# Gate and up projections of two 768-token feed-forwards as seven half products each, with the down projection cut into pieces between them

## The chip, the cores and the metric

The program runs on one core of one Trainium2 chip. The metric is the time of one execution on the device, in microseconds (us); lower is better. The core has TensorE (PE in the rows; its weight loads are PEld), VectorE (DVE), ScalarE (ACT), GpSimd (POOL) and the queue SP, from which most transfers are issued.

## What is computed

The reference is two blocks of two layers each over 512 tokens of width 1024, with 256 context tokens beside them. Each of the four layers ends in a feed-forward of hidden width 2816:

```python
def swiglu(h, w_in, w_out):
    g, u = jnp.split(h @ w_in, 2, axis=-1)
    return (jax.nn.silu(g) * u) @ w_out
```

In the first layer of each block the kernel runs the feed-forward over the 512 tokens and the 256 context tokens together (768 columns); in the second layer of each block over 512. All arithmetic is float32.

## The kernel before, in words

Activations lie with the model dimension on the 128 partitions: eight tiles of 128 x tokens. A float32 product is made of three passes of TensorE: each operand is split into a rounded part `hi` and the rest `lo`, and `mm3` adds hi·hi, hi·lo (of the activations) and lo·hi (of the weights) into one accumulator in PSUM. `segs` cuts 768 columns into a matmul of 512 and one of 256, each with its own weight load.

The hidden width is 22 chunks of 128. For a chunk c, `ffn` calls `chunk` twice (gate and up): `wload` transfers 128 x 1024 weights into a `wraw` tile (4 buffers), ScalarE writes `whi` (L298) and GpSimd `wlo` (L299; 3 buffers each), and 8 x 3 x 2 matmuls follow (L306, L308, L310). Then ScalarE makes silu of the gate (L683), VectorE multiplies it by the up result in PSUM (L684), and `split` makes the hidden pair (L334 on ScalarE, L335 on VectorE). Chunks stand in groups, two in the first and four in each of five others. After the first chunk of the next group, `down` multiplies a group's hidden pairs by its rows of the down projection: one `wload` holds 8 blocks of 128 x 128, and each of the 8 output tiles takes 6 matmuls for each hidden chunk and is then added into the residual by VectorE (L574, one instruction for 512 columns and one for 256). PSUM gives three accumulators of two banks (`pd`); two more banks (`pq`) are for small things.

During these feed-forwards VectorE also computes the modulation vectors of the next layer (`ada`, L372): 48 weight tiles go through the same `wraw` buffers, with one or two multiply-and-sum instructions each, doled out by `fill.pace()`.

The order of the instructions of an engine is made by a list scheduler: the order in the program is the priority, and a later instruction may go first when it is ready earlier. On the chip each engine keeps that order.

Of the kernel before, what the change touches and what calls it, by code (L numbers as in the profile page):

```python
# [21 lines left out]
P = 128  # L22
# [195 lines left out]
class Kern:  # L218
# [110 lines left out]
    def split(self, src, n, lo_eng=None, pool=None):  # L329
# [301 lines left out]
    def ffn(self, x, wg, wu, wo, h, m, g, n, st, norm, fill, parts):  # L631

        nc = self.nc
        hp = self.es.enter_context(self.tc.tile_pool(name=self.nm("hid"), bufs=8, reuse_waits="tile"))
        oi = 0
        end = len(FGROUPS) - 1

# [35 lines left out]
        before = None  # L673
        for gi, grp in enumerate(FGROUPS):
            hid = []
# [469 lines left out]
    def ffn_block(self, a, win, wout, l, h, m, g, n, st, norm, fill=None, parts=None):  # L1145
        wi, wo = self.I[win], self.I[wout]
        self.ffn(a, lambda c: wi[l * 44 + c], lambda c: wi[l * 44 + 22 + c], lambda c: wo[l * 22 + c], h, m, g, n, st, norm, fill or Fill(), parts)

# [11 lines left out]
    def layer0(self):  # L1160
# [4 lines left out]
        with ExitStack() as es:  # L1165
            self.psum(es, pd=1, sc=2)
            w = I["even_w_in"]
            with self.tc.tile_pool(name="raw", bufs=6, reuse_waits="tile") as pool:
                a, ws = self.first_modulated(job, load, [w[8], w[12], w[16]], pool)
            for n in ("lamv", "cos", "sin", "sguw", "sgub"):  # L1170
                self.nc.sync.dma_start(getattr(self, n), I[n])
            self.ada_vectors(0)
            y = self.even_mixer(a, ws)
            st, h, a = self.stat(T, False), [], self.pairs()
            norm = self.rms_modulated(a, h, T, st, "norm2_g0", m, 24, 32)
            self.out_proj(I["even_w_out"], y, [4, 5, 6, 7, 0, 1, 2, 3], load, m, 16, T, h, st, norm)
            self.dump("hm0", h, T)
        with ExitStack() as es:
            self.psum(es, pd=3)
            st, b = self.stat(T, False), self.pairs()  # L1180
# [6 lines left out]
    def layer1(self, h, a, job):  # L1187
# [12 lines left out]
        with ExitStack() as es:  # L1200
            self.psum(es, pd=3)
            st = self.stat(NL, False)
# [668 lines left out]
    def second(self, h, st, job):  # L1871
# [3 lines left out]
        with self.es2 as es0:  # L1875
# [9 lines left out]
            with ExitStack() as es:  # L1885
                self.psum(es, pd=3)
                job = self.ada_start(1, 1)
# [18 lines left out]
            with ExitStack() as es:  # L1906
                self.psum(es, pd=3)
                st = self.stat(NL, True)
# [49 lines left out]
    def block1(self):  # L1958
        nc, tc, I = self.nc, self.tc, self.I
        with ExitStack() as es:  # L1960
# [5 lines left out]
            self.sin = self.t(bc, [P, NL], "sin")  # L1966
            self.sguw = self.t(bc, [P, 4, P], "sguw")
            self.sgub = self.t(bc, [P, 4, P], "sgub")
            self.lamv = self.t(bc, [64, 4], "lamv")
# [10 lines left out]

def lay_out(w):
    out = []
    w4 = w.reshape(-1, P, KC, P)
    for grp in FGROUPS:
        nk = len(grp)
# [48 lines left out]
def layout(x):  # L2034
# [11 lines left out]
    a["ffn_w_in"] = np.concatenate([lay_in(f["ffn_w_in"][l]) for l in range(2)])  # L2046
    a["ffn_w_out"] = np.concatenate([lay_out(f["ffn_w_out"][l]) for l in range(2)])
    a["cos"], a["sin"] = rope_tables()
# [72 lines left out]
```

## Time and profile before

| what | value |
|---|---|
| median of 3 runs | 4047.41 us (4041.08 to 4049.92) |
| the profiled execution | 4058.61 us, its span 4056.8 us |
| mean granted clock of TensorE | 0.944 of full speed |
| TensorE busy | 3690.5 us, 91% of the span |
| VectorE, GpSimd, ScalarE busy | 55%, 34%, 33% |
| feed-forward of 768 tokens, first block | from about 461 to 1020 us of the span |
| the same, second block | from about 2640 to 3200 us |

Busy time of an engine is the time in which an instruction of it runs; matmuls are pipelined, so their spacing, not their duration, says how fast they go. The rows below are from the profiled execution, and its numbers stand against its own 4058.61 us, which is 11 us above the median.

### The profile page before, as it was taken

The page shows a single profiled execution, that of the slowest core. Times are in us where ns is not written, and L with a number is a line of the kernel's source. Part 1 is how long each engine was busy: PE and PEld are TensorE (multiplying, and loading weights), DVE is VectorE, ACT ScalarE, POOL GpSimd, SP SyncE. Part 2 cuts the span into 40 slices and gives each one's busy share as a digit, 9 for nine tenths or more (in the row PEclk, how much of TensorE's full clock was granted, in tenths as well). Part 3 has the DMA queues.
Part 4 walks back from the last instruction along what each step waited for, and adds up shares of the span by engine and source line. Part 5 has one row for each costly group of instructions (what it writes and reads, how often), then busy time and mean ns, then how long its engine had stood idle before and what let it go on. Part 6 is the DMA issues. An engine that isn't in the chain of part 4 may idle for free.

```text
span 4056.8 us, 57267 instructions
## 1 busy us (share of the span) xinstructions
PE 3690.5 (91%) x22809; PEld 3065.6 (76%) x22809; DVE 2233.0 (55%) x4199; ACT 1347.2 (33%) x2337; POOL 1388.1 (34%) x804
## 2 busy tenths in 40 slices
PE   6989999999799899998977869699999899989997
PEld 4777788888677778776755657688888777778886
DVE  4784554333776676646767664755333654364225
ACT  5542212112466222243332322331111365543222
POOL 2112322222312444432332224552222542245443
PEclk9999999999899999989886879899999899999998
DMA  5124134333101255424445768223333221222331
GB/s 194 37 96 155 56 104 129 119 113 118 48 27 53 89 181 172 151 82 129 125 135 154 220 185 278 81 68 120 115 119 121 77 64 60 61 73 78 94 99 57
DMA packets 263002, 450.18 MB, mean 111 GB/s; under 512 B 63504, under 2 KB 168592, under 8 KB 259664
## 3 DMA queue, kind: packets, MB, share of 16 engines
q1 hardware_dynamic: 257536, 424.50, 33.7%
q10 hardware_dynamic: 5200, 22.02, 1.6%
q8 instruction: 180, 2.95, 0.3%
q14 instruction: 86, 0.70, 0.1%
HBM read 383.02 MB, written 63.44 MB: 110 GB/s over the span
## 4 chain that ended last, share of the span: by engine, by line
PE 38%; DVE 7%; DMA 2%; ACT 2%; issue 1%; POOL 1%; SPq 0%; ACTq 0%; DVEq 0%; POOLq 0%
PE pd L310 9%; PE pd L306 9%; PE pd L308 9%; PE pq L982 1%; DVE s L181 1%; DVE h L171 1%; PE ch L1756 1%; POOL s L1491 1%; PE sc L1135 1%; PE c L1513 1%; PE pq L997 1%; PE ch L1743 1%; PE sc L1138 1%; DVE h L557 0%; DMA lf<-ldd 0%
## 5 line engine op out<-in xcount | busy, mean ns | idle before, releaser
L299 POOL TENSOR_TENSOR wlo<-wraw,whi 128x1024 fp32r<-128x1024 f32 (+2 forms) x406 | 937.5, 2311 | 1916.8 <-ACT whi L298 1801.7
L306 PE MATMUL pd<-s,whi 128*128 128x512 f32 (+1 forms) x3481 | 1055.1, 356 | 37.4 <-ACT s L509 10.0
L308 PE MATMUL pd<-s,whi 128*128 128x512 f32 (+1 forms) x3421 | 1044.8, 356 | 14.7 <-DVE s L510 6.4
L310 PE MATMUL pd<-s,wlo 128*128 128x512 f32 (+1 forms) x3481 | 1053.3, 354 | 1.6 <-POOL wlo L299 1.6
L298 ACT CAST whi<-wraw 128x1024 fp32r<-128x1024 f32 (+2 forms) x414 | 405.6, 981 | 1627.3 <-PE pd L308 924.9
L306 PEld LDWEIGHTS pd<-s,whi 128*128 128x128 f32 x3481 | 585.9, 191 | 141.4 <-ACT s L509 12.2
L310 PEld LDWEIGHTS pd<-s,wlo 128*128 128x128 f32 x3481 | 589.7, 191 | 94.1 <-POOL wlo L299 3.5
L308 PEld LDWEIGHTS pd<-s,whi 128*128 128x128 f32 x3421 | 577.1, 191 | 109.5 <-DVE s L510 9.7
L372 DVE SCALAR_TENSOR_TENSOR junk<-wraw,cond 128x1024 bf16<-128x1024 f32 x160 | 263.8, 1649 | 395.5 <-DMA wraw<-in_ada_w 395.2
L574 DVE SCALAR_TENSOR_TENSOR h<-pd,mod,h 128x512 f32<-128x512 f32 (+1 forms) x323 | 196.2, 636 | 200.8 <-PE pd L310 200.4
L684 DVE TENSOR_TENSOR s<-s,pd 128x768 f32<-128x768 f32 (+1 forms) x88 | 71.9, 817 | 344.5 <-PE pd L310 310.3
L306 PE MATMUL pd<-hid,whi 128*128 128x512 f32 (+1 forms) x624 | 194.8, 350 | 4.9 <-DVE h L574 4.2
L308 PE MATMUL pd<-hid,whi 128*128 128x512 f32 (+1 forms) x624 | 194.0, 348 | 1.2 <-DVE hid L335 1.2
L310 PE MATMUL pd<-hid,wlo 128*128 128x512 f32 (+1 forms) x624 | 192.9, 347 | 0.0
L954 DVE TENSOR_REDUCE negm<-sc 128x1 f32<-128x512 f32 (+1 forms) x128 | 96.3, 754 | 118.3 <-PE sc L1135 107.4
L372 DVE SCALAR_TENSOR_TENSOR wraw<-wraw,cond 128x1024 f32<-128x1024 f32 x96 | 129.1, 1345 | 4.0
L306 PEld LDWEIGHTS pd<-hid,whi 128*128 128x128 f32 x624 | 110.4, 193 | 22.5 <-DVE h L574 2.4
L308 PEld LDWEIGHTS pd<-hid,whi 128*128 128x128 f32 x624 | 110.8, 194 | 16.3 <-DVE hid L335 1.7
L306 PE MATMUL pd<-in,whi 128*128 128x256 f32 (+1 forms) x384 | 114.0, 363 | 9.9 <-DVE h L1228 7.9
L310 PEld LDWEIGHTS pd<-hid,wlo 128*128 128x128 f32 x624 | 110.9, 194 | 15.3
L181 DVE TENSOR_TENSOR s<-s,s 128x256 f32<-128x256 f32 (+2 forms) x106 | 101.4, 957 | 37.6 <-ACT s L180 36.2
L308 PE MATMUL pd<-in,whi 128*128 128x256 f32 (+1 forms) x384 | 114.3, 365 | 2.9 <-POOL in L510 1.9
(375 smaller groups left out, 5761.6 us busy)
## 6 DMA issues: line engine op xcount, KB each, us to landing
wraw<-in_ada_w SPq DMA_DIRECT2D x160, 512.0 KB, 3.6
wraw<-in_ffn_w SPq DMA_DIRECT2D x132, 512.0 KB, 3.6
wraw<-in_ffn_w_in SPq DMA_DIRECT2D x88, 512.0 KB, 3.6
wraw<-in_ffn_w_out SPq DMA_DIRECT2D x44, 512.0 KB, 3.6
recd<-xr SPq DMA_DIRECT2D x72, 256.0 KB, 2.9
rec<-recd ACTq DMA_DIRECT2D x12, 1536.0 KB, 7.8
rec<-recd SPq DMA_DIRECT2D x12, 1536.0 KB, 7.0
raw<-in_ada_w SPq DMA_DIRECT2D x32, 512.0 KB, 5.8
```

The lines of the kernel that those rows point to most:

```text
L171: nc.vector.tensor_tensor(out=x[:, a:b], in0=x[:, a:b], in1=self.shift[:, a:b], op=ALU.subtract)
L181: nc.vector.tensor_tensor(out=self.sq[:, a:b], in0=self.sq[:, a:b], in1=t[:, a:b], op=ALU.add)
L298: nc.scalar.copy(hi, raw)
L299: (lo_eng or nc.gpsimd).tensor_tensor(out=lo, in0=raw, in1=hi.bitcast(F32), op=ALU.subtract)
L306: nc.tensor.matmul(ps[:, o:o + b - a], lhsT=whi, rhs=xhi[:, a:b], start=start, stop=False)
L308: nc.tensor.matmul(ps[:, o:o + b - a], lhsT=whi, rhs=xlo[:, a:b], start=False, stop=False)
L310: nc.tensor.matmul(ps[:, o:o + b - a], lhsT=wlo, rhs=xhi[:, a:b], start=False, stop=stop)
L372: nc.vector.scalar_tensor_tensor(raw if r else self.junk, raw, 1.0, self.cond[r], op0=ALU.mult, op1=ALU.mult, accum_out=m[:, j, r:r + 1])
L574: nc.vector.scalar_tensor_tensor(h[k][:, x:y], ps[:, x - o:y - o], m[:, g + k, r:r + 1], h[k][:, x:y], op0=ALU.mult, op1=ALU.add)
L684: nc.vector.tensor_tensor(out=sl[:, :n], in0=sl[:, :n], in1=pu[:, :n], op=ALU.mult)
L954: nc.vector.tensor_reduce(nm, ps[:, base:T], axis=AX.X, op=ALU.max, negate=True)
L982: nc.tensor.transpose(pt[:, (i - a) * P:(i - a + 1) * P], pe[:, pos[i]:pos[i] + P], self.ident)
```

## The change

Only the two feed-forwards of 768 tokens change; those of 512 go through `ffn_plain`, which is the old code. Chunks 0 and 1 are still computed whole. For the other 20, gate and up of a chunk are taken as a 2 x 2 block product: two halves of the 1024 inputs by (gate, up) on the weights' side, two halves of 384 tokens by two halves of the inputs on the activations' side. It is made of seven products of half size (Winograd's form of Strassen's scheme), each of 4 x 3 matmuls of 384 columns, in place of eight. The sums of activations that this takes are made once for a feed-forward (`half_sums`); those of the weights once for a chunk (four subtractions or additions of 128 x 512 on VectorE), and the results are put together by seven additions of 128 x 384. Each half-size weight operand gets its own `hi` on ScalarE and `lo` on GpSimd (`wop`).

Groups now have two chunks (the last one four). The down projection of the group before is a generator that gives one output tile at each of four places of a pair of gate and up; it has one accumulator (`sf`, two banks), and the products four single banks (`sb`). The two tables of the first mixer (`sguw`, `sgub`) move to a pool that is closed before the feed-forward.

```diff
-FGROUPS = [[0, 1], [2, 3, 4, 5], [6, 7, 8, 9], [10, 11, 12, 13], [14, 15, 16, 17], [18, 19, 20, 21]]
+FGROUPS = ([[c, c + 1] for c in range(0, 18, 2)] + [[18, 19, 20, 21]],
+           [[0, 1]] + [list(range(c, c + 4)) for c in range(2, 22, 4)])
...
+    def wop(self, src):
+        nc = self.nc
+        if self.wsl is None:
+            self.wsl = self.t(self.wp, [P, 1024], "whi", F32R), self.t(self.wp, [P, 1024], "wlo", F32R)
+            (hi, lo), r = self.wsl, slice(0, 512)
+        else:
+            (hi, lo), r = self.wsl, slice(512, 1024)
+            self.wsl = None
+        nc.scalar.copy(hi[:, r], src)
+        nc.gpsimd.tensor_tensor(out=lo[:, r], in0=src, in1=hi[:, r].bitcast(F32), op=ALU.subtract)
+        return hi[:, r], lo[:, r]
+
+    def mmh(self, ps, w, x):
+        mm, (hi, lo) = self.nc.tensor.matmul, w
+        for i, (a, b) in enumerate(x):
+            k = slice(i * P, (i + 1) * P)
+            mm(ps, lhsT=hi[:, k], rhs=a, start=i == 0, stop=False)
+            mm(ps, lhsT=hi[:, k], rhs=b, start=False, stop=False)
+            mm(ps, lhsT=lo[:, k], rhs=a, start=False, stop=i == 3)
+
+    def half_sums(self, x, n, hp):
...
+        def put(dst, src, eng):
+            nc.scalar.copy(dst[0], src)
+            eng.tensor_tensor(out=dst[1], in0=src, in1=dst[0].bitcast(F32), op=ALU.subtract)
+            return dst
...
+        for i in range(4):
+            (h1, l1), (h2, l2) = ((x[0][k][:, :n], x[1][k][:, :n]) for k in (i, i + 4))
+            y1, y2 = (self.t(hp, [P, T], "hid")[:, :n] for _ in range(2))
+            if i % 2 == 0:
+                z = self.t(hp, [P, T], "hid")[:, :n]
+            t = z[:, b if i % 2 else a]
+            G.tensor_tensor(out=y1, in0=h1.bitcast(F32), in1=l1.bitcast(F32), op=ALU.add)
+            V.tensor_tensor(out=y2, in0=h2.bitcast(F32), in1=l2.bitcast(F32), op=ALU.add)
+            V.tensor_tensor(out=y1[:, a], in0=y1[:, b], in1=y1[:, a], op=ALU.subtract)
+            V.tensor_tensor(out=t, in0=y2[:, b], in1=y1[:, b], op=ALU.subtract)
+            V.tensor_tensor(out=y2[:, b], in0=y2[:, b], in1=y1[:, a], op=ALU.subtract)
+            V.tensor_tensor(out=y2[:, a], in0=y2[:, a], in1=y2[:, b], op=ALU.subtract)
...
+            ops["t2"].append(put(half(), y2[:, b], V))
+            ops["t1"].append(put(half(), y1[:, a], G))
+            ops["t4"].append(put(half(), y2[:, a], V))
+            t3.append((h1, l1, t))
+        for i, (h1, l1, t) in enumerate(t3):
+            ops["t3"].append(put((h1[:, b], l1[:, b]), t, (V, G)[i % 2]))
...
     def ffn(self, x, wg, wu, wo, h, m, g, n, st, norm, fill, parts):
...
+        def down(hid):
...
+            for f0 in range(0, KC, nf):
+                hl = self.wload(wo(oi))
+                oi += 1
+                for f in range(nf):
+                    ps = self.ps("sf")
+                    for kc in range(nk):
+                        self.mm3(ps, *hl[f * nk + kc], xs[0][kc], xs[1][kc], kc == 0, kc == nk - 1, self.segs(n))
+                    done(f0 + f, ps, 0, n)
+                    if f == nf - 1:
+                        fill.pace()
+                    yield
...
+        def pair(c, between):
+            V, A = nc.vector, nc.scalar
+            rg, ru = (self.t(self.wp, [P, 1024], "wraw") for _ in range(2))
+            nc.sync.dma_start(rg, wg(c))
+            nc.sync.dma_start(ru, wu(c))
...
+            def product(w, name):
+                ps = self.t(self.pp, [P, 512], "sb")[:, :H]
+                self.mmh(ps, self.wop(w), ops[name])
+                return ps
+
+            A.copy(sl[:, ha], product(g1, "a1"))
+            q = product(g2, "a2")
+            V.tensor_tensor(out=s3, in0=g1, in1=u1, op=ALU.subtract)
+            V.tensor_tensor(out=u1, in0=u1, in1=u2, op=ALU.add)
+            V.tensor_tensor(out=g1, in0=u1, in1=g1, op=ALU.subtract)
+            V.tensor_tensor(out=g2, in0=g2, in1=g1, op=ALU.subtract)
+            between.step()
+            add(sl[:, hb], sl[:, ha], product(g1, "t2"))
+            add(sl[:, ha], sl[:, ha], q)
+            add(up[:, ha], sl[:, hb], product(s3, "t3"))
+            between.step()
+            q = product(u1, "t1")
+            add(up[:, hb], up[:, ha], q)
+            add(sl[:, hb], sl[:, hb], q)
+            add(up[:, ha], up[:, ha], product(u2, "t4"))
+            between.step()
+            add(sl[:, hb], sl[:, hb], product(g2, "b2"))
+            A.activation(sl, sl, AF.Silu)
+            V.tensor_tensor(out=sl, in0=sl, in1=up, op=ALU.mult)
+            fill.pace()
+            between.step()
+            return self.split(sl, n, pool=hp)
...
+        ops = self.half_sums(x, n, hp)
+        with ExitStack() as e2:
+            self.psum(e2, sb=4, sf=1)
+            for grp in FGROUPS[0][1:]:
+                between = Fill(down(hid))
+                hid = [pair(c, between) for c in grp]
+                between.drain()
+        with ExitStack() as e3:
+            self.psum(e3, pd=3)
+            down_last(hid)
```

## Rows read from the trace of the kernel before

**Rows 1.** Page, parts 1 and 2: busy time; tenths of 40 slices

```profile
PE 3690.5 (91%) x22809; PEld 3065.6 (76%) x22809; DVE 2233.0 (55%) x4199; ACT 1347.2 (33%) x2337; POOL 1388.1 (34%) x804
PE   6989999999799899998977869699999899989997
```

**Rows 2.** Windows: us, then busy (x instructions) PE, PEld, DVE, ACT, POOL, clock, DMA

```profile
500.00:1000.00 500.00, 500.00 (x2833) 434.03 (x2832) 200.22 (x259) 95.74 (x102) 145.09 (x59) 1.00 0.37 116
2680.00:3180.00 500.00, 500.00 (x2843) 434.66 (x2842) 195.53 (x265) 93.74 (x100) 146.38 (x59) 1.00 0.36 114
```

**Rows 3.** Timeline, PE: start, us; runs of 256 columns alone, then 512 alone

```profile
480.49 0.28 PE L306 MATMUL pd<-s,whi 128*128 128x256 f32 x1
480.61 0.28 PE L308 MATMUL pd<-s,whi 128*128 128x256 f32 x1
...
1001.59 0.39 PE L308 MATMUL pd<-hid,whi 128*128 128x512 f32 x1
1001.82 0.39 PE L310 MATMUL pd<-hid,wlo 128*128 128x512 f32 x1
```

**Rows 4.** Groups by shape, 500 to 1000 us: busy, mean ns, idle before

```profile
L299 POOL TENSOR_TENSOR wlo<-wraw,whi 128x1024 fp32r<-128x1024 f32 x59 | 145.1, 2459 | 352.3 <-ACT whi L298 352.3
L372 DVE SCALAR_TENSOR_TENSOR junk<-wraw,cond 128x1024 bf16<-128x1024 f32 x48 | 76.3, 1589 | 154.0 <-DMA wraw<-in_ada_w 154.0
L298 ACT CAST whi<-wraw 128x1024 fp32r<-128x1024 f32 x59 | 61.9, 1048 | 358.4 <-PE pd L308 212.5 <-issue 139.3 <-PE pd L310 6.6
L574 DVE SCALAR_TENSOR_TENSOR h<-pd,mod,h 128x512 f32<-128x512 f32 x41 | 30.7, 749 | 57.9 <-PE pd L310 57.9
L684 DVE TENSOR_TENSOR s<-s,pd 128x768 f32<-128x768 f32 x21 | 20.0, 950 | 72.5 <-PE pd L310 72.5
L372 DVE SCALAR_TENSOR_TENSOR wraw<-wraw,cond 128x1024 f32<-128x1024 f32 x16 | 19.6, 1225 | 1.0
L574 DVE SCALAR_TENSOR_TENSOR h<-pd,mod,h 128x256 f32<-128x256 f32 x40 | 19.0, 475 | 0.0
L683 ACT ACTIVATE s<-pd 128x768 f32<-128x768 f32 x20 | 16.1, 805 | 0.0
```

**Rows 5.** The same view, 440 to 490 us (512 columns) and whole trace (384)

```profile
L529 DVE TENSOR_TENSOR s<-h,s 128x512 f32<-128x512 f32 x8 | 6.6, 821 | 0.0
L181 DVE TENSOR_TENSOR s<-s,s 128x512 f32<-128x512 f32 x1 | 0.7, 693 | 0.7 <-ACT s L180 0.7
L509 ACT CAST s<-s 128x512 fp32r<-128x512 f32 x8 | 5.0, 620 | 15.8 <-DVE s L530 15.8
L510 POOL TENSOR_TENSOR s<-s,s 128x512 fp32r<-128x512 f32 x4 | 5.5, 1376 | 14.9 <-ACT s L509 14.9
...
L880 DVE TENSOR_TENSOR big<-pq,big 128x384 fp32r<-128x384 f32 x32 | 17.1, 546 | 0.6 <-ACT big L879 0.4
```

**Rows 6.** Timeline of DVE and POOL at two places of the two feed-forwards

```profile
518.32 2.39 POOL L299 TENSOR_TENSOR wlo<-wraw,whi 128x1024 fp32r<-128x1024 f32 x1 [6.08 <-ACT whi L298]
519.43 2.10 DVE L335 TENSOR_TENSOR hid<-s,hid 128x768 fp32r<-128x768 f32 x1 [0.90 <-ACT hid L334]
...
2672.03 7.81 POOL L299 TENSOR_TENSOR wlo<-wraw,whi 128x1024 fp32r<-128x1024 f32 x3 [5.27 <-ACT whi L298]
2672.69 0.95 DVE L684 TENSOR_TENSOR s<-s,pd 128x768 f32<-128x768 f32 x1 [8.85 <-ACT s L683]
```

**Rows 7.** Timeline, DVE, second feed-forward, where the split stands free

```profile
2855.89 0.96 DVE L335 TENSOR_TENSOR s<-s,s 128x768 fp32r<-128x768 f32 x1 [0.90 <-ACT s L334]
```

**Rows 8.** Timeline, start of the first feed-forward: DVE, POOL, PE

```profile
485.22 0.41 DVE L510 TENSOR_TENSOR s<-s,s 128x256 fp32r<-128x256 f32 x1
485.82 0.74 POOL L510 TENSOR_TENSOR s<-s,s 128x256 fp32r<-128x256 f32 x1 [0.67 <-ACT s L509]
491.75 0.62 PE L306 MATMUL pd<-s,whi 128*128 128x512 f32 x2 [2.42 <-ACT s L683]
500.61 0.95 DVE L684 TENSOR_TENSOR s<-s,pd 128x768 f32<-128x768 f32 x1 [4.62 <-PE pd L310]
502.47 2.10 DVE L335 TENSOR_TENSOR s<-s,s 128x768 fp32r<-128x768 f32 x1 [0.91 <-ACT s L334]
```

**Rows 9.** Windows, PE and clock, two stretches with gaps in the matmuls

```profile
486.00:492.00 6.00, 3.58 (x29) 3.37 (x29) 0.27 (x1) 3.44 (x4) 2.90 (x2) 1.00 0.00 0
1020.00:1030.00 10.00, 5.91 (x42) 0.83 0.29 95
```

More of the change, by code (lines that the diff above doesn't have):

```diff
@@ L633, in ffn, with done, done_last @@
         nc = self.nc
+        es = self.es
+        hp = es.enter_context(self.tc.tile_pool(name=self.nm("hid"), bufs=8, reuse_waits="tile"))
+        sp = es.enter_context(self.tc.tile_pool(name=self.nm("half"), bufs=1, reuse_waits="tile"))
+        BUFS.update(hid=8, s3=1, up=1, sb=4, sf=1)
+        H = n // 2
+        ha, hb = slice(0, H), slice(H, n)
+        oi = 0
+        self.wsl = None
+        def done(f, ps, a, b):
+            self.residual_add(h, ps, f, m, g, a, b)
+        def done_last(f, ps, a, b):
+            done(f, ps, a, b)
+            st.add(h[f], a, b)
@@ new lines, in down_last @@
+        def down_last(hid):
+            nonlocal oi
+            nk = len(hid)
+            nf = 8 // nk
+            xs = [a for a, _ in hid], [b for _, b in hid]
+            fill.drain()
+            late = []
+            for f0 in range(0, KC, nf):
+                hl = self.wload(wo(oi))
+                oi += 1
+                if f0 >= KC - LAST * nf:
+                    late += [(f0 + f, hl[f * nk:(f + 1) * nk]) for f in range(nf)]
+                    continue
+                pss = [self.pd() for _ in range(nf)]
+                for k0, k1 in ((0, nk - 1), (nk - 1, nk)):
+                    for f in range(nf):
+                        hf = hl[f * nk:(f + 1) * nk]
+                        for kc in range(k0, k1):
+                            self.mm3(pss[f], *hf[kc], xs[0][kc], xs[1][kc], kc == 0, kc == nk - 1, self.segs(n))
+                        if k1 == nk:
+                            done_last(f0 + f, pss[f], 0, n)
+            self.by_parts(late, xs, n, done_last, norm)
@@ new lines, in ffn @@
+        with ExitStack() as e1:
+            self.psum(e1, pd=3)
+            first = self.chunks([wg(0), wu(0), wg(1)], x, n, parts=parts or self.parts(n))
+            self.flush()
+            hid = []
+            for c in range(2):
+                pg = first[2 * c]
+                pu = first[1] if c == 0 else self.chunk(wu(c), x, n)
+                sl = self.s()
+                nc.scalar.activation(sl[:, :n], pg[:, :n], AF.Silu)
+                nc.vector.tensor_tensor(out=sl[:, :n], in0=sl[:, :n], in1=pu[:, :n], op=ALU.mult)
+                hid.append(self.split(sl, n, pool=hp))
+                fill.pace()
@@ L673, in ffn @@
         before = None
-        for gi, grp in enumerate(FGROUPS):
+        for gi, grp in enumerate(FGROUPS[1]):
             hid = []
@@ L1200, in layer1 @@
         with ExitStack() as es:
-            self.psum(es, pd=3)
+            self.es = es
             st = self.stat(NL, False)
@@ L1978, in lay_in, with lay_out @@
     return w.reshape(k // P, P, f // P, P).transpose(2, 1, 0, 3).reshape(f // P, P, k)
-def lay_out(w):
+def lay_out(w, groups):
     out = []
     w4 = w.reshape(-1, P, KC, P)
-    for grp in FGROUPS:
+    for grp in groups:
         nk = len(grp)
```

48 lines of the change are left out of this document (39 added, 9 removed).

## The prediction

> **What bounds the kernel now.** I read the page first: TensorE is busy 91% of the span, no other engine over 55%, and the slices show where it is not full [rows 1]. Then the windows over the two feed-forwards of 768 tokens: in 1000 us TensorE has no idle time at all, at a granted clock of 1.00 (the upper level, 2.4 GHz), while VectorE is busy 40%, GpSimd 29%, ScalarE 19% [rows 2]. So these stages are bound by TensorE alone, and every other engine waits for it: GpSimd idles 352 us of 500 before its weight remainders, ScalarE 212 us for TensorE to release weight buffers [rows 4]. A matmul less is time less here, as long as the cover lasts.
>
> The price of a matmul: 2833 and 2843 in 500 us each [rows 2], that is 1000/5676 = 0.1762 us. These are half of 512 and half of 256 columns, so 384 in the mean. Alone, 256 columns follow each other every 0.12 us and 512 every 0.23 us [rows 3]; a line through the two gives 0.175 at 384. The weight load that goes with each is hidden at 256 columns already, so it is at 384. Bounds for a 384-column matmul are 0.12 and 0.23; I take 0.176, as its work lies half way.
>
> **The change, part by part.**
>
> *Removed on TensorE.* Gate and up of a chunk were 2 x 8 x 3 x 2 = 96 matmuls; now 7 x 4 x 3 = 84 of the same mean size. The down projection keeps its count (8 outputs x 6 for each chunk, 48). So 12 for each of 20 chunks, 240 x 0.1762 = 42.3 us in a feed-forward, **84.6 us in both**. A chunk with its share of the down projection falls from 144 x 0.1762 = 25.4 to 132 x 0.1762 = 23.3 us.
>
> *Added on VectorE*, per chunk. Seven additions of 384 columns with one operand in PSUM: 0.546 us each [rows 5], 3.8. Four weight sums of 512 columns, both operands in SBUF: 0.69 each (the one free row; 0.82 in the mean of eight) [rows 5], 2.8. The product with silu: 0.95 as before [rows 4]. The split: 0.96 when free [rows 7]. Residual additions: groups of two mean 8 outputs for each two chunks, each 0.749 + 0.475 [rows 4], 4.9 a chunk where it was 2.45. Over the 20 chunks (9 groups with a down part in between): 76 + 55 + 19 + 19 + 72 x 1.224 = 88, sum 257 us. The modulation vectors take 76 + 20 and some 10 of small things [rows 4], 106. Together 363 us, against a TensorE time of 20 x 84 + 18 x 48 = 2544 matmuls, 448 us; before, 200 in 500.
>
> *What VectorE loses to GpSimd.* A split that starts at 519.43 while GpSimd works until 520.71 takes 2.10 us, as if it began when GpSimd ended; the same instruction alone takes 0.96; the product with an operand in PSUM runs at its 0.95 inside a GpSimd stretch [rows 6, 7]. GpSimd's work grows: 7 remainders of 512 columns (1.38 each in the rows, 1.23 as half of a 2.46 one; I take 1.28) and 0.9 of the down projection's 2.46 for a chunk [rows 4, 5], 7 x 1.28 + 2.2 = 11.2 of 23.3 us, where it was about 7 of 25.4. Of six instructions a chunk with both operands in SBUF (four sums, the product, the split), a share 0.39 meets a short one with 0.64 us to go in the mean, and 0.1 a long one with 1.23: 0.37 us each, 45 us over 120. VectorE stands at 363 + 45 = 408 of 448 us, 91%. It is not the bound, but a queue that full, in a fixed order, is late now and then. The lower bound of this loss is 0 (GpSimd never in the way), the upper 1.28 for each, 154 us. The Trainium skill, SBUF — State Buffer, section Who interferes with whom, says that an instruction of VectorE with two inputs in SBUF and one of GpSimd that reads SBUF shut each other out for the whole instruction. By that rule the upper bound is real wherever the two start together.
>
> *Where lateness costs.* The down accumulator is single. Between the third and the fourth down piece of a chunk lies one product, 12 x 0.176 = 2.1 us, in which VectorE has to finish 0.749 + 0.475 us of residual addition; there is 0.9 us of room, and one modulation instruction (1.23 to 1.59) or a blocked sum ahead of it in the queue uses that up. I take 0.5 us a chunk, 10 us a feed-forward; bounds 0 and 1.6 (a whole such instruction). At the border of a group, the next down piece needs the split of the chunk just finished: addition 0.55, silu 0.8, product 0.95, two splits 0.84 and 0.96, with waits some 4.5 us, and 1.2 of residual addition and 1.3 of modulation in the same queue, 7 us; a fourth down piece and two products, 6.3 us, and its own first half, 1 us, cover that. With one or two blocked instructions it is late by 0.4 to 1.6: I take 0.6 at 9 borders, 5 us. So 15 us a feed-forward, **30 in both**; bounds 0 and 2 x (32 + 14) = 92.
>
> *The start.* The activations are complete at about 486 us [rows 8], and TensorE ends the last whole chunk at about 500.6. Then the products a1 and a2 need no sums, and with one down piece they last 6.3 us; t2 starts at about 508. Until then `half_sums` must go through: for each of four steps VectorE has 0.96 + 4 x 0.55 + 2 x 0.55, 4.3 us, 17 us in all and about 3 for the last pass, with 0.95 + 0.96 twice for chunks 0 and 1 in between [rows 8], some 24 us from 486, plus blocking by GpSimd's 13 us. That ends at 510 to 516; the first step's result is wanted first and comes early. I take 6 us of waiting (bounds 0 and 10) and 1 for the accumulators that change hands, when product L684 still reads one [rows 8]: 7 a feed-forward, **14 in both**.
>
> *Costed at nothing.* Weight transfers are as many as before, and their buffers are held longer; what hides them is that ScalarE waits up to 7 us for buffers now. ScalarE: 140 casts of 0.62 for 40 of 1.05 [rows 4, 5], with silu and the splits some 150 of 448 us. The moved tables: two loads behind the first weight chunks. The last group waits for its split as before, behind the first three quarters of two outputs (36 matmuls, 6.3 us). If one of these covers were gone, a landing of 3 to 4 us would show once for each.
>
> *Sum.* -84.6 + 30 + 14 = -40.6 us on the profiled 4058.61, so 4018; the median of the runs stands 11 us lower, so **4007**.
>
> **Rivals.**
>
> *The forecast* (0.50): TensorE stays the bound, waits of about 0.75 us a chunk. 3980 to 4030.
>
> *All is covered* (0.14): VectorE at 91% needs no room, the sums arrive. Only the two starts remain, some 4 us: 4047 - 80 = 3967. For it: TensorE had no wait at all under a queue of 40%. Against it: the 91%.
>
> *VectorE sets the first half, no change* (0.16): the modulation work was drawn into the first 200 us of the 500. If it is again packed into 10 chunks, VectorE has (257 + 45)/20 + 10.6 = 25.7 us a chunk there, against 23.3: 24 us a feed-forward instead of 5 of the waits above, total -40.6 + 38 = -3, 4045. Against it: two raw weight tiles are now held through a chunk, so the modulation tiles get fewer of the four buffers.
>
> *The lock makes VectorE the bound throughout, slower* (0.17): if the 120 instructions lose more than 1.07 us each, VectorE needs more than the 492 us that 20 chunks took before, (491 - 363)/120. At 1.28 it needs 517: 69 us over TensorE, so -84.6 + 14 + 138 = +67, 4115. For it: 2.10 against 0.96, and that the weight sums run just when GpSimd makes the first remainders of the same chunk. Against it: chance starts give 0.37, and VectorE would need to run without a pause.
>
> *The clock* (0.03): short waits at each product. A gap of 2.42 us before a matmul left the granted clock at 1.00, a stretch with TensorE busy 5.91 of 10 us has 0.83 [rows 8, 9]. If both feed-forwards went at 0.83, 448/0.83 would be 92 us more in each: 4190. In the rows only the long gaps go with a low clock. The Trainium skill, TensorE: Matmul & The Clock Gate, section A second HAM failure mode: psum-queue depth-cycling, describes a kernel whose many short waits between accumulators make the clock swing; by it this case would be likelier than I put it, and no row here shows that.
>
> **How the numbers follow.** The measurement tells 0.2%, 8 us, from no change. Faster: 0.50 + 0.14 and a quarter of the third case, 0.68. Same: 0.10. Slower: the fourth and fifth and the rest, 0.22. The range goes from 3962, below the covered case, to 4062: it takes in the no-change case and the part of the slower one near its threshold, and leaves out some 0.03 below and 0.15 above. The forecast's own is 3980 to 4030.
>
> **What would show it.** Matmuls of 384 columns every 0.175 us; 480 fewer matmuls in all; VectorE's busy share in both stages at 80 to 90%; idle time of TensorE there some 22 us a feed-forward, most of it before the fourth down piece (released by L574's successor) and before the first t2. Wrong if 384 columns cost near 0.23, if TensorE waits for weight operands (ScalarE or GpSimd as releaser) instead, or if the weight sums last near 2 us.

## The result and the profile after

| kernel | median of 4 runs, us | lowest to highest | profiled execution | its span |
|---|---|---|---|---|
| before | 4044.24 | 4040.39 to 4049.92 | 4058.61 | 4056.8 |
| after | 4068.07 | 4062.72 to 4072.01 | 4067.65 | 4065.9 |

The ratio is 1.0057, with a 95% interval of 1.0038 to 1.0075. The change makes the kernel slower by some 23 us (15 to 30); the forecast was 4007, and 4068 lies above its range of 3962 to 4062. The two profiled executions differ by 9 us only, since that of before is 14 above its median and that of after stands at its own.

Page of after, parts 1 and 2, beside [rows 1]:

```profile
PE 3624.0 (89%) x22329; PEld 3065.1 (75%) x22329; DVE 2675.9 (66%) x4827; ACT 1455.8 (36%) x2609; POOL 1675.6 (41%) x1024
...
PE   6989889999789899988977879679999899989997
```

The matmuls are 22809 - 22329 = 480 fewer, as forecast, and the time is longer all the same: TensorE now waits. To see where, both traces are cut at the last weight transfer of each mixer's output projection, which stands ahead of each feed-forward. Timeline of the transfer queue, before, then after (start, us of the issue):

```profile
401.46 0.33 SPq L295 DMA_DIRECT2D wraw<-in_even_w_out  x1
...
1305.02 0.33 SPq L295 DMA_DIRECT2D wraw<-in_odd_w_out  x1
...
2588.26 4.43 SPq L295 DMA_DIRECT2D wraw<-in_ev_w_out  x2
...
3605.04 0.33 SPq L295 DMA_DIRECT2D wraw<-in_od_w_out  x1
```

```profile
402.19 0.33 SPq L296 DMA_DIRECT2D wraw<-in_even_w_out  x1
...
1314.25 0.33 SPq L296 DMA_DIRECT2D wraw<-in_odd_w_out  x1
...
2590.41 4.43 SPq L296 DMA_DIRECT2D wraw<-in_ev_w_out  x2
...
3613.89 0.33 SPq L296 DMA_DIRECT2D wraw<-in_od_w_out  x1
```

From the ends of these rows, the stretch of the first changed feed-forward goes from 903.6 to 912.1 us (+8.5), that of the second from 1012.7 to 1019.4 (+6.7), and the middle one, whose code is unchanged, from 1287.3 to 1280.3. So each changed feed-forward lost 42.3 us of matmuls (240 x 0.1762) and took up about 50 us of waits and slower matmuls, where 22 was forecast.

Windows of after, beside [rows 2] (PE, PEld, DVE, ACT, POOL busy with counts, clock, DMA share, GB/s):

```profile
500.00:520.00 20.00, 12.42 (x60) 10.07 (x58) 13.79 (x16) 5.33 (x10) 12.74 (x8) 0.83 0.09 28
520.00:540.00 20.00, 13.65 (x48) 10.57 (x49) 18.36 (x28) 7.05 (x14) 10.02 (x8) 0.65 0.07 25
540.00:600.00 60.00, 54.15 (x305) 50.70 (x304) 46.87 (x71) 16.13 (x25) 33.26 (x20) 0.99 0.30 97
600.00:700.00 100.00, 92.77 (x511) 86.86 (x511) 87.76 (x122) 27.36 (x43) 54.89 (x31) 0.97 0.36 116
...
900.00:1000.00 100.00, 96.78 (x552) 92.26 (x551) 74.92 (x111) 32.82 (x52) 58.92 (x37) 1.00 0.43 135
2680.00:2700.00 20.00, 14.55 (x78) 12.20 (x76) 16.71 (x14) 5.35 (x11) 13.16 (x9) 0.95 0.15 50
2700.00:2720.00 20.00, 11.02 (x32) 7.39 (x32) 19.11 (x25) 5.83 (x13) 12.18 (x9) 0.63 0.09 26
```

Two losses are to be seen. In the 40 us from 500 on, TensorE does 108 matmuls, 19 us of work, so 21 us are lost (and 40 - 110 x 0.1762 = 20.6 in the second feed-forward). After that it runs short by a few per cent everywhere: it does 2448 matmuls from 540 to 1000, 431 us of work in 460. Waits of TensorE, 500 to 1005 and, the last row, 2670 to 3200 us (us in total, times, longest):

```profile
PE sf L307 <- DVE h L642: 23.9, 21, 2.5
PE sb L357 <- ACT s L376: 7.6, 2, 4.8
PE sb L358 <- POOL s L377: 2.3, 2, 1.7
...
PE sf L309 <- DVE hid L336: 0.9, 1, 0.9
...
PE sf L307 <- DVE h L642: 26.9, 22, 2.5
```

The steady loss is the single down accumulator `sf`: TensorE waits for VectorE's residual addition (L642) to empty it. L376 and L377 are `half_sums`, the start. Of the 21 us lost there, 14 are waits (of these rows and three smaller ones); the other 7 go with a granted clock of 0.83 and 0.65.

### The profile page after: what moved, and what is told of

It is laid out like the page before. It is cut to its first block, busy times and chain, and to the rows that moved or that the text cites. A ratio compares the mean times of both kernels' runs of the same rounds, so it can differ in the third digit from the quotient of the medians.

```text
span 4065.9 us, 57730 instructions
## 1 busy us (share of the span) xinstructions
PE 3624.0 (89%) x22329; PEld 3065.1 (75%) x22329; DVE 2675.9 (66%) x4827; ACT 1455.8 (36%) x2609; POOL 1675.6 (41%) x1024
## 5 line engine op out<-in xcount | busy, mean ns | idle before, releaser
L307 PE MATMUL pd<-s,whi 128*128 128x512 f32 (+1 forms) x1881 | 644.5, 370 | 38.0 <-ACT s L577 9.5
L309 PE MATMUL pd<-s,whi 128*128 128x512 f32 (+1 forms) x1821 | 628.2, 369 | 14.6 <-DVE s L578 6.2
L311 PE MATMUL pd<-s,wlo 128*128 128x512 f32 (+1 forms) x1881 | 637.9, 365 | 1.6 <-POOL wlo L300 1.6
L349 POOL TENSOR_TENSOR wlo<-wraw,whi 128x512 fp32r<-128x512 f32 x240 | 377.9, 1591 | 264.9 <-ACT whi L348 264.9
L307 PEld LDWEIGHTS pd<-s,whi 128*128 128x128 f32 x1881 | 341.6, 194 | 104.2 <-issue 14.0
L357 PE MATMUL sb<-s,whi 128*128 128x384 f32 x1120 | 378.3, 338 | 15.1 <-ACT s L376 11.9
L309 PEld LDWEIGHTS pd<-s,whi 128*128 128x128 f32 x1821 | 332.6, 193 | 74.5 <-DVE s L578 10.1
L358 PE MATMUL sb<-s,whi 128*128 128x384 f32 x1120 | 378.3, 338 | 10.8 <-DVE s L377 6.2
L311 PEld LDWEIGHTS pd<-s,wlo 128*128 128x128 f32 x1881 | 342.4, 193 | 56.1 <-POOL wlo L300 3.5
L359 PE MATMUL sb<-s,wlo 128*128 128x384 f32 x1120 | 376.8, 336 | 0.0
L440 DVE SCALAR_TENSOR_TENSOR junk<-wraw,cond 128x1024 bf16<-128x1024 f32 x160 | 275.0, 1719 | 112.8 <-DMA wraw<-in_ada_w 112.3
L357 PEld LDWEIGHTS sb<-s,whi 128*128 128x128 f32 x1120 | 212.2, 190 | 25.1 <-ACT s L376 14.3
L358 PEld LDWEIGHTS sb<-s,whi 128*128 128x128 f32 x1120 | 211.9, 189 | 15.4 <-DVE s L377 9.4
L359 PEld LDWEIGHTS sb<-s,wlo 128*128 128x128 f32 x1120 | 211.8, 189 | 0.0
L307 PE MATMUL sf<-hid,whi 128*128 128x512 f32 x576 | 154.8, 349 | 50.9 <-DVE h L642 50.9
L642 DVE SCALAR_TENSOR_TENSOR h<-sf,mod,h 128x512 f32<-128x512 f32 (+1 forms) x288 | 163.7, 607 | 10.8 <-PE sf L311 10.8
L642 DVE SCALAR_TENSOR_TENSOR h<-pd,mod,h 128x512 f32<-128x512 f32 (+1 forms) x163 | 105.3, 658 | 89.0 <-PE pd L311 88.7
L309 PE MATMUL sf<-hid,whi 128*128 128x512 f32 x576 | 150.7, 342 | 1.8 <-DVE hid L336 1.8
```

Source lines behind the costliest of these rows:

```text
L307: nc.tensor.matmul(ps[:, o:o + b - a], lhsT=whi, rhs=xhi[:, a:b], start=start, stop=False)
L309: nc.tensor.matmul(ps[:, o:o + b - a], lhsT=whi, rhs=xlo[:, a:b], start=False, stop=False)
L311: nc.tensor.matmul(ps[:, o:o + b - a], lhsT=wlo, rhs=xhi[:, a:b], start=False, stop=stop)
L349: nc.gpsimd.tensor_tensor(out=lo[:, r], in0=src, in1=hi[:, r].bitcast(F32), op=ALU.subtract)
L357: mm(ps, lhsT=hi[:, k], rhs=a, start=i == 0, stop=False)
L358: mm(ps, lhsT=hi[:, k], rhs=b, start=False, stop=False)
```

## The experiments

All were compared with the kernel before on the same chip. Two theories stood against each other for the steady waits: that VectorE is simply too full (its load), or that instructions with both operands in SBUF, blocked while GpSimd works, make the residual late (the lock). For the start: that the sums begin too late, or that they are slowed. The modulation work (L440 in after) is on VectorE all through: 47 us of it from 550 to 700, where it is densest, and 53 from 700 to 1000.

**The rest of the kernel** (`e1_plain`). Both feed-forwards through the old code; only the moved tables and the order of other things remain.

```diff
...
-        (self.ffn if n == T else self.ffn_plain)(a, lambda c: wi[l * 44 + c], lambda c: wi[l * 44 + 22 + c], lambda c: wo[l * 22 + c], h, m, g, n, st, norm, fill or Fill(), parts)
+        self.ffn_plain(a, lambda c: wi[l * 44 + c], lambda c: wi[l * 44 + 22 + c], lambda c: wo[l * 22 + c], h, m, g, n, st, norm, fill or Fill(), parts)
```

> Both feed-forwards of 768 tokens go through the old code; what is left of the change is the move of two small tables and of the accumulators' pool. If all of the loss lies inside the two feed-forwards (theory), the time is that of the kernel before, 4044 within 8 us. If part of it lies outside them (rival: the two traces differ by +9, -7 and +9 us in three places), 4050 to 4060.

4050.01 us, ratio 0.9994 (0.9976 to 1.0011): no difference within that interval, so the loss lies in the two feed-forwards, and costing the moved tables at nothing was right.

**The start without its sums** (`e2_no_act_sums`). The seven products take plain halves of the activations.

```diff
-        ops = self.half_sums(x, n, hp)
+        op = lambda k0, r: [(x[0][k][:, r], x[1][k][:, r]) for k in range(k0, k0 + 4)]
+        ops = dict(a1=op(0, ha), a2=op(4, ha), b2=op(4, hb), t1=op(0, ha), t2=op(4, hb), t3=op(0, hb), t4=op(4, ha))
```

> The sums of the activations are left out (the seven products read the plain halves; the output is not the reference's). Start theory: in the first 40 us TensorE lost 21 us in each feed-forward, 7 to 10 of them in waits for these sums and most of the rest because its granted clock fell to 0.5 to 0.65 behind them; without them 2 x 17 to 20 us go, 4068 to about 4030. Rival, the waits in the steady part come to the same place anyway (VectorE has 20 us less to do, but the chunks still queue): 4055 to 4065.

4029.04 us, 0.9943 (0.9917 to 0.9969), that is 1.0057 - 0.9943 = 1.14% or 46 us (some 13 either way, from the two intervals) under after for both starts. Windows of this kernel:

```profile
500.00:520.00 20.00, 18.86 (x109) 17.92 (x108) 10.37 (x18) 5.88 (x10) 8.41 (x7) 1.00 0.16 54
520.00:540.00 20.00, 18.36 (x106) 17.19 (x106) 14.10 (x19) 5.29 (x8) 10.92 (x7) 1.00 0.22 79
```

215 matmuls where after has 108, at a clock of 1.00. The wait for the down accumulator stays at 24.3 us: the two losses are separate.

**The sums called earlier** (`e3_early`). The loop over the activations stands ahead of chunks 0 and 1.

```diff
...
+            hs = self.half_sums(x, n, hp)
+            ops = next(hs)
             hid = []
...
-        ops = self.half_sums(x, n, hp)
+        next(hs, None)
```

> The first part of the sums of the activations is called before chunks 0 and 1 are finished, so that its tiles are taken first; only the third operand, which overwrites the activations, stays where it was. Theory: the sums began at 506 us and not at 487 because their tiles came behind the hidden pair of chunk 1 in one pool of eight; called early they hide behind the last whole chunk, and 10 to 18 us go in each feed-forward: 4032 to 4048. Rival, VectorE and GpSimd are the limit of the sums, not their start: less than 5 us in each, 4058 to 4068.

4071.67 us, 1.0053 (1.0033 to 1.0072): nothing won. The sums ran from 489, but TensorE has one wait of 23.6 us in their place. Its row, then the timeline of ScalarE:

```profile
PE pd L307 <- ACT s L811: 23.6, 1, 23.6
```

```profile
515.79 0.51 ACT L376 CAST s<-hid 128x384 fp32r<-128x384 f32 x1 [0.88 <-DVE hid L394]
516.68 0.51 ACT L376 CAST s<-hid 128x384 fp32r<-128x384 f32 x1 [0.37 <-DVE hid L391]
...
518.50 0.81 ACT L811 ACTIVATE s<-pd 128x768 f32<-128x768 f32 x1
```

The silu of chunk 0, which frees an accumulator, stands in ScalarE's queue behind the casts of the sums, each of which waits for VectorE. The data would have allowed the early start; the queues, in a fixed order, made it as dear as the late one.

**One ring of six banks** (`e4_ring`). Products and down pieces share six single banks, so a down piece can begin before the one ahead of it is emptied.

```diff
...
-                    ps = self.ps("sf")
+                    p2 = [self.t(self.pp, [P, 512], "sb") for _ in range(2)]
...
-            self.psum(e2, sb=4, sf=1)
+            self.psum(e2, sb=6)
```

> The down projection and the products share one ring of six single banks; a down piece takes two. Theory: TensorE waited 24 and 27 us for the residual addition to release the one down accumulator; with banks in turn 15 to 25 us of that go in each feed-forward: 4020 to 4038. Rival, VectorE is late by its load (80 to 90 in 100 busy, and blocked by GpSimd), so that the wait only moves to the products' banks: 4055 to 4068.

4048.66 us, 0.9989 (0.9972 to 1.0007), 0.7% under after, between theory and rival. From 700 to 800 us TensorE goes from 536 matmuls to 570, but in the 50 us from 600 on only 212 are done, with a wait of up to 4.3 us for the residual: where the modulation work is densest, VectorE is too late for six banks too. In its profile the two feed-forwards gain only 3.5 and 1.7 us and the unchanged middle stretch 11.5, so most of what the median gains isn't explained by the trace.

**The weight sums left out** (`e5_no_w_sums`). The products take the weight halves as loaded; VectorE has four instructions fewer a chunk.

```diff
...
-            V.tensor_tensor(out=s3, in0=g1, in1=u1, op=ALU.subtract)
-            V.tensor_tensor(out=u1, in0=u1, in1=u2, op=ALU.add)
-            V.tensor_tensor(out=g1, in0=u1, in1=g1, op=ALU.subtract)
-            V.tensor_tensor(out=g2, in0=g2, in1=g1, op=ALU.subtract)
...
```

> The four weight sums of each chunk on VectorE are left out (the products read the raw halves; the output is not the reference's). Load theory: in the steady part TensorE waits 24 us a feed-forward because VectorE, with 80 to 90 of 100 us busy, comes late to the residual additions; without the sums it has 4.1 of 23 us less to do for each chunk, and 15 us or more of the 24 go in each feed-forward: 4040 to 4052 beside 4068 for the changed kernel. Rival, the distance of one product between the third and fourth down piece sets the wait, whatever the load: less than 6 us in each, 4058 to 4068.

4025.86 us, 0.9946 (0.9926 to 0.9966). The wait for the down accumulator falls from 23.9 to 11.8 us (14.8 in the second feed-forward). In the first, all that is left lies before 700 us, where the modulation work is densest; from 700 to 900 there are 1155 matmuls in 200 us, 0.173 each. The time is below even the 4040 to 4052 of the load theory. By itself this fits the load and the lock.

**The remainders off GpSimd** (`e6_lo_on_act`). VectorE has exactly the work of after; ScalarE writes the low parts of the product weights, as plain copies, and GpSimd keeps only those of the down projection.

```diff
         nc.scalar.copy(hi[:, r], src)
-        nc.gpsimd.tensor_tensor(out=lo[:, r], in0=src, in1=hi[:, r].bitcast(F32), op=ALU.subtract)
+        nc.scalar.copy(lo[:, r], src)
```

> The remainders of the seven products' weights are not computed by GpSimd; ScalarE writes a copy in their place (the output is not the reference's). GpSimd is then nearly free, and VectorE's own work is as before. Lock theory: the instructions of VectorE with two operands in SBUF get their free durations (weight sums 0.69 instead of 0.87 to 1.19 us, split 0.96 instead of 1.63), some 2.5 us for each chunk, and the waits of 24 us a feed-forward fall by half: 4040 to 4055. Rival, the number of VectorE's instructions sets the waits: 4060 to 4068.

3996.29 us, 0.9885 (0.9853 to 0.9916). The waits row, a window, and the groups by shape from 540 to 1000 us:

```profile
PE sf L307 <- DVE h L642: 1.5, 4, 0.6
```

```profile
700.00:800.00 100.00, 100.00 (x579) 95.72 (x578) 74.80 (x117) 46.47 (x78) 12.05 (x5) 1.00 0.42 131
```

```profile
L795 DVE TENSOR_TENSOR s<-s,up 128x768 f32<-128x768 f32 x20 | 32.7, 1637 | 15.7 <-ACT s L794 15.7
...
L782 DVE TENSOR_TENSOR wraw<-wraw 128x512 f32<-128x512 f32 x18 | 12.3, 686 | 2.0 <-ACT wlo L349 2.0
```

The gain is far larger than the 4040 to 4055 expected. With the same count of VectorE instructions the wait is gone, 1.5 us for 23.9 (0.4 for 26.9 in the second), and VectorE is still 84% busy from 600 to 700 us: load alone is not the cause. The sums go at 0.69 us, where after needs 0.87 to 1.19. The product with silu still meets GpSimd's remaining work, 1.64 us in the mean against 1.14 in after, and so does the split, 1.53 against 1.63, not the 0.96 expected; with so little waiting left, that costs TensorE next to nothing. Beside the lock a second thing changed: the low parts come from a shorter instruction (0.62 us for 1.60), so the sums that overwrite raw weights are released sooner. By the rows that part is the smaller one: L781 and L782 wait 14.4 us for GpSimd in after and 7.8 for ScalarE's low parts here, where the four sums take 26 us longer in after than free. No run takes the two apart, so what is shown is that GpSimd's remainders make the wait, by both ways together.

**The weight sums on GpSimd** (`e7_w_sums_pool`). `V` becomes `nc.gpsimd` in the four lines that e5 removes.

> The four weight sums are made by GpSimd instead of VectorE. Load theory: VectorE falls to some 65% busy, GpSimd rises from 56% to about 80%, and the waits for the down accumulator fall from 24 to some 12 us a feed-forward: 4045 to 4058. Rival, GpSimd becomes the late one (it has 11 us of remainders and 5 to 6 of sums in 23 us, and the sums stand in front of the remainders that TensorE needs): TensorE waits for weight operands, slower than the changed kernel, above 4075.

4128.49 us, 1.0208 (1.0191 to 1.0226). VectorE is busy 56 to 59% from 700 to 900 us, and the wait for the accumulator rises to 40.5 us in 17 pieces (41.2 in the second feed-forward). That looks like the lock, but the trace gives another reason. Timeline, VectorE and TensorE:

```profile
845.78 1.46 DVE L440 SCALAR_TENSOR_TENSOR junk<-wraw,cond 128x1024 bf16<-128x1024 f32 x1 [7.05 <-DMA wraw<-in_ada_w]
...
848.57 1.13 DVE L642 SCALAR_TENSOR_TENSOR h<-sf,mod,h 128x512 f32<-128x512 f32 x2
...
849.75 1.01 PE L307 MATMUL sf<-hid,whi 128*128 128x512 f32 x2 [3.70 <-DVE h L642]
```

VectorE stands idle for 7.05 us at the head of its queue for a modulation tile that hasn't landed; the residual is behind it. There are 79 us of such idle time from 500 to 1005, where after has 16; most likely the tile is late because GpSimd's sums hold the raw weight buffers longer. The run says nothing on the lock. It shows a late transfer ahead of the residual doing what a blocked sum does. It isn't the whole loss: the two waits rose by 31 us, the time by 61 over after. From 540 to 1000 us TensorE loses 58 us beside its matmuls (29 in after), of which 40 are waits, and its granted clock is 0.95 there (0.99 in after).

**Two more whole chunks as cover** (`e8_hidden_start`). Chunks 2 and 3 stay whole; the sums run beside them. In this run and the next four, `s3` and `up` also share two buffers with a tile of the sums.

```diff
...
+            for c in (2, 3):
+                ops = next(hs)
+                pg, pu = (self.chunk(w(c), x, n) for w in (wg, wu))
...
-            for grp in FGROUPS[0][1:]:
+            for grp in FGROUPS[0][2:]:
```

> Chunks 2 and 3 are computed whole too, with down pieces after each, and the sums of the activations are made in their shadow; 18 chunks go by halves. Start theory: 4.2 us more of matmuls in each feed-forward, but of the 23 us of the start 15 to 20 go: 4038 to 4050 beside 4068. Rival, the sums on VectorE and GpSimd (some 30 us with the lock) delay the whole chunks as they did when called early: 4060 or more.

4052.97 us, 1.0012 (0.9995 to 1.0028), short of the theory's 4038 to 4050. From 500 to 540 there are 217 matmuls, none lost; the next 60 us have 265 where after had 305, and 600 to 700 has 481 for 511. VectorE does the same bulk in the same queue and is late afterwards: of some 19 us won, 12 (70 matmuls) come back by 700. The stretches (910.1 and 1019.2) hardly move, though the median is 0.45% under after; that gap is open.

**Fewer chunks in halves** (`e9_whole_to_9`, `e10_whole_to_9_ring`, `e11_whole_to_13_ring`, `e12_fine`). Chunks 0 to 9 are whole, while the dense part of the modulation work and the sums go through; then come halves. e10 adds the ring of e4, e11 is e10 with chunks 0 to 13 whole, e12 is e10 with the sums in four steps (after chunks 3, 5, 7, 8) rather than two.

```diff
...
+            for grp in FGROUPS[0][1:5]:
...
+                    if c in (4, 6):
+                        ops = next(hs)
...
-            for grp in FGROUPS[0][1:]:
+            for grp in FGROUPS[0][5:]:
```

> Chunks 0 to 9 are computed whole, with the sums of the activations doled out after chunks 4 and 6; chunks 10 to 21 by halves. VectorE has room in whole chunks, and the modulation work is over by then, so the steady part costs 0.18 us a matmul as it did between 700 and 1000 us: 12 chunks x (25.4 - 23.9) = 18 us won, 3 to 8 lost at the change-over: 10 to 15 us a feed-forward against the kernel before, 4020 to 4030 beside 4047. Rival, the sums cost 20 us at the change-over wherever they stand, as in the two runs that moved them: 4045 to 4060.

> The same with the ring of six banks for the halves. If the ring helps where VectorE is not loaded by the modulation work (570 matmuls in 100 us against 536 in one stretch): 12 chunks x (25.4 - 23.3) = 25 us won, 15 to 20 net in each feed-forward, 4007 to 4020. If not, as the run without it, 4020 to 4030.

> Chunks 0 to 13 whole, 14 to 21 by halves, with the ring. If the gain is proportional to the chunks taken by halves: 8 x 2.1 = 17 us less 3 to 5, 12 us a feed-forward, 4020 to 4027. If the change-over is the larger cost: within 8 us of the kernel before.

> As the run with chunks 0 to 9 whole and the ring, but the sums of the activations are doled out in four steps, after chunks 3, 5, 7 and 8, in place of two. In that run TensorE waited 10.7 us in the first feed-forward, in three waits, for the product with silu of a whole chunk that stood in VectorE's queue behind two steps of the sums. If half a block of sums is short enough to be taken up by the chunk's own slack: 5 us or more won in each feed-forward, 4015 to 4025. Rival, each step costs its wait and there are now four: 4032 to 4040.

| kernel | median, us | ratio | interval |
|---|---|---|---|
| e9, no ring | 4061.06 | 1.0035 | 1.0023 to 1.0048 |
| e10 | 4031.77 | 0.9969 | 0.9957 to 0.9981 |
| e11 | 4030.14 | 0.9956 | 0.9938 to 0.9973 |
| e12 | 4029.19 | 0.9945 | 0.9927 to 0.9963 |

All four came out above what their first theory gave, e9 by some 30 us: in its first feed-forward it still waits 11.9 us for the down accumulator and 10.1 for silu products of whole chunks, against 25 us of matmuls saved. In the same 50 us (850 to 900), e9 has 274 matmuls and e10 286, 0.182 and 0.175 each: where the modulation work is thinner, six banks cover the late residual. e10 to e12 beat both kernels, at the price of leaving 8 to 12 of the 20 chunks whole; their intervals overlap, so the three aren't clearly told apart. Of the 288 matmuls that e12 saves (50.7 us), 22 us remain. In the first feed-forward of e10 three waits of 10.7 us in all are for the silu product of a whole chunk, behind the sums; in e12 those are 5.2, and four for a residual make 7.4.

**The start without the lock** (`e13_sums_on_vector`). All activation sums on VectorE.

```diff
-        V, G = nc.vector, nc.gpsimd
+        V = G = nc.vector
```

> The changed kernel with all sums of the activations on VectorE; GpSimd keeps only the remainders of the weights. VectorE has 4 x 1.8 = 7 us more of its own work in each start (24 in place of 17), and GpSimd 13 us less. Lock theory: the start is long because the two engines shut each other out (2.0 to 2.3 us for instructions of 0.95, 1.3 to 1.8 for those of 0.55); alone VectorE is done after some 24 to 26 us in place of 27, and the start loses 2 to 6 us less: 4056 to 4066. Rival, the bulk of VectorE's work sets the start: 5 to 7 us more in each, 4078 to 4084.

4062.39 us, 1.0029 (1.0015 to 1.0044), 0.28% or 11 us under after. Every sum now lasts 0.55 or 0.95 us, and the block goes from 507.7 to 529.7, 22 us, where after takes from 510.8 to 538.2. But the 40 us of the start have 118 matmuls for 108, and the second start, counted from the same place in both, 117 for 109: 3 us for both starts. So the block's length and its late beginning are the cost, and doing without the lock takes some 5 us off the block. The rest of the 11 us isn't in these rows; the profiled execution was 13 us above this kernel's median, so its stretches add nothing.

## Why the prediction was wrong, step by step

Two terms of the sum were too small: the down accumulator (20 us for both feed-forwards, measured 50.8) and the start (14, measured 41.6, over its own upper bound). The border of a group was too large (10, measured 1.8).

*What was right.* 480 matmuls went, and those of 384 columns follow each other as forecast: timeline of after, VectorE, GpSimd and TensorE around one chunk's third and fourth down piece:

```profile
844.78 2.56 POOL L349 TENSOR_TENSOR wlo<-wraw,whi 128x512 fp32r<-128x512 f32 x2 [3.69 <-ACT whi L348]
...
846.08 0.34 PE L357 MATMUL sb<-s,whi 128*128 128x384 f32 x1
846.25 0.33 PE L358 MATMUL sb<-s,whi 128*128 128x384 f32 x1
...
846.12 1.77 DVE L782 TENSOR_TENSOR wraw<-wraw 128x512 f32<-128x512 f32 x1 [0.71 <-POOL wlo L349]
847.81 1.13 DVE L642 SCALAR_TENSOR_TENSOR h<-sf,mod,h 128x512 f32<-128x512 f32 x2
...
849.00 0.62 PE L307 MATMUL sf<-hid,whi 128*128 128x512 f32 x2 [0.67 <-DVE h L642]
```

From 846.08 to 846.25 is 0.17 us, so the term of -84.6 stands. The place of the wait was right too: one product between two pieces, the residual late behind a blocked sum. L782 starts at 846.12 while GpSimd works until 847.34, and takes 1.77 us instead of 0.69; those 1.08 us are more than the 0.67 that TensorE then waits. Without them this wait wouldn't be, nor without the 0.71 us for which L782 stands waiting for the remainder just before.

*The loss of VectorE: the mean was right.* Groups by shape of after, 540 to 1000 us, beside [rows 4]:

```profile
L440 DVE SCALAR_TENSOR_TENSOR junk<-wraw,cond 128x1024 bf16<-128x1024 f32 x48 | 73.5, 1532 | 16.1 <-DMA wraw<-in_ada_w 16.1
...
L770 DVE TENSOR_TENSOR s<-s,sb 128x384 f32<-128x384 f32 x78 | 42.6, 546 | 0.7
...
L336 DVE TENSOR_TENSOR hid<-s,hid 128x768 fp32r<-128x768 f32 x19 | 31.0, 1632 | 2.0 <-ACT hid L335 1.7
...
L782 DVE TENSOR_TENSOR wraw<-wraw 128x512 f32<-128x512 f32 x19 | 22.6, 1191 | 3.6 <-POOL wlo L349 3.6
...
L795 DVE TENSOR_TENSOR s<-s,up 128x768 f32<-128x768 f32 x19 | 21.7, 1140 | 11.8 <-ACT s L794 11.8
```

The additions from PSUM cost the forecast 0.546. The four weight sums mean 0.96, 1.11, 0.87 and 1.19 us, 26 us over 0.69 in the feed-forward; the split 1.63 for 0.96 and the product 1.14 for 0.95 make 16 more: 42 us, where 45 was forecast, and VectorE is busy 75 to 88% in the windows above, near the 80 to 90 that were said. The Trainium skill, SBUF — State Buffer, section Who interferes with whom, states that an instruction of VectorE with two inputs in SBUF and one of GpSimd that reads SBUF exclude each other. The trace agrees: 1.77 us above, where L782 ends 0.55 us after GpSimd does, and 0.69 once GpSimd is out of the way.

*The step that failed first: the down accumulator.* "I take 0.5 us a chunk" was 10 us a feed-forward; measured 23.9 and 26.9, inside the bound of 32 and far from the value taken. The forecast spread the mean loss evenly; with 0.9 us of room it counts where in the queue it falls. In the first feed-forward the waits come in two sizes: to 704 us, where the modulation work is densest, most are 1.4 to 2.5; after that most are 0.6 to 0.7, once a chunk, a steady pattern and not a chance one. Of the 41 in both steady parts, 18 stand behind a blocked L782 as above (1.65 to 1.77 us). Another 18 stand behind an L782 that is free, the last 5 behind modulation instructions alone. One of those behind a free L782, timeline of after, VectorE and TensorE:

```profile
867.33 1.63 DVE L440 SCALAR_TENSOR_TENSOR junk<-wraw,cond 128x1024 bf16<-128x1024 f32 x1 [0.58 <-DMA wraw<-in_ada_w]
...
871.06 0.68 DVE L782 TENSOR_TENSOR wraw<-wraw 128x512 f32<-128x512 f32 x1
871.66 1.13 DVE L642 SCALAR_TENSOR_TENSOR h<-sf,mod,h 128x512 f32<-128x512 f32 x2
...
872.85 0.62 PE L307 MATMUL sf<-hid,whi 128*128 128x512 f32 x2 [0.62 <-DVE h L642]
```

Here the lateness comes from further up: VectorE hasn't paused since 867.33, and that stretch opens with a modulation instruction of 1.63 us, which takes 1.22 in e6, after 0.58 of waiting for its tile. e6 shows that without GpSimd's remainders both kinds go, e4 and e10 that more accumulators absorb the small ones and not the large. The border of a group, forecast at 5 us, was one wait of 0.9.

*The step that failed second: the start.* The forecast had the sums run "some 24 us from 486" and end at 510 to 516, 7 us of waiting. Timeline of after, GpSimd, VectorE, TensorE, beside [rows 8]:

```profile
505.92 4.08 POOL L389 TENSOR_TENSOR hid<-s,s 128x768 f32<-128x768 f32 x2
...
510.75 0.94 DVE L390 TENSOR_TENSOR hid<-s,s 128x768 f32<-128x768 f32 x1
...
528.03 1.78 DVE L393 TENSOR_TENSOR hid<-hid,hid 128x384 f32<-128x384 f32 x1
...
524.92 0.52 PE L359 MATMUL sb<-s,wlo 128*128 128x384 f32 x1
525.24 0.52 PE L357 MATMUL sb<-s,whi 128*128 128x384 f32 x1
```

They take 27 us, but begin at 506 to 511: in the program they come behind chunk 1, and so do their tiles in a pool that they share with its hidden pair. e3 shows that 489 was possible, and that it then costs elsewhere. So the overlap was wrong: the sums don't run beside the last whole chunk, and TensorE waits 11 us for them where 6 were taken, 10 at most (14 with the accumulators that change hands, a border and a residual). And a term was put at nothing: TensorE, with 48 matmuls in 20 us, has a granted clock of 0.65 of full speed (between its levels of 1.2 and 2.4 GHz), and its few matmuls come every 0.32 us in place of 0.17; the other 7 us go with that. Measured: 21 us a feed-forward, and 46 (some 13 either way) for both by e2.

*The sum.* From the traces: 84.6 saved, the starts (21.0 + 20.6), the accumulator (23.9 + 26.9).

| kernel | saved | both starts | accumulator | sum | measured (interval) |
|---|---|---|---|---|---|
| after | -84.6 | 41.6 | 50.8 | +8 | +23 (+15 to +30) |
| e2 | -84.6 | 4.9 | 48.5 | -31 | -23 (-34 to -13) |
| e5 | -84.6 | 39.5 | 26.6 | -19 | -22 (-30 to -14) |
| e6 | -84.6 | 34.7 | 1.9 | -48 | -47 (-59 to -34) |
| e7 | -84.6 | 44.4 | 81.7 | +42 | +84 (+77 to +92) |

Measured is the ratio less 1 by the median of before; the starts are 40 us less the matmuls in them by 0.1762, in windows shifted with the first half product of each trace (0.8 us of a start's waits in after stands in both columns). The sums of e2, e5 and e6 lie inside their intervals. That of after is 7 us short of the nearer end: its profile shows +15.2 in the two stretches, some 2 of it because the last whole chunk ends at 503.1 rather than 500.6, a few in short waits and in the clock of 0.99. That of e7 gives half of the loss; in the first feed-forward some 18 us beside its waits go with the clock of 0.95. What is left beyond that is open, as is the unchanged middle stretch, which lies between 1264 and 1287 us in the profiles of this study.

*The rivals.* None came true as told. The lock does not make VectorE the bound throughout: TensorE is 91 to 97% busy in the steady parts. The modulation work does make the first half worse (511 matmuls from 600 to 700, 552 from 900 to 1000), as the rival of no change had it; but its premise holds in part only, since in before, too, 39 of the 96 us of that work lie after 700. In after the clock fell much in the start alone; from 600 on it is 0.97 to 1.00 under some 20 short waits. In e7, with 17 waits of up to 6.0 us, it is 0.95 from 540 to 1000. The Trainium skill, TensorE: Matmul & The Clock Gate, section A second HAM failure mode: psum-queue depth-cycling, describes short waits between accumulators that make the clock swing. The trace of after doesn't show that for waits of 0.4 to 2.5 us.

## What to carry to other kernels

An engine that is 85% busy in a fixed order isn't priced by its mean: find the wait with the least room (here 0.9 us before a single accumulator), list what stands ahead of it in the queue, back to the engine's last pause, and give each its blocked duration, not its mean. Work that is needed once (22 us of sums) is better laid beside work that doesn't need it, with an eye on every queue it touches; whether in two steps or four made no clear difference here (e10, e12). A fraction of a saving taken where the second engine has room (e12, 0.55%) beats all of it taken everywhere.

## What the runs showed of the hardware that was not expected

The lock costs both sides: GpSimd's remainder of 512 columns lasts 1.28 us when nothing is in its way, and 1.60 (of raw weights) and 1.93 (of the sum s3) in the mean of the steady part. It was also already in rows of before that were taken for free ones: the modulation instruction of [rows 4] at 1.59 us takes 1.22 in e6 with GpSimd nearly idle.
